# Weights-times-values products of even and odd key blocks accumulated in the two halves of the PSUM partitions

## The chip, the cores and the metric

One core of a Trainium2 chip runs the whole program. The metric is device time in microseconds (us) of one execution; the lower the better.

## The reference

One layer of a hybrid encoder trunk over 2048 positions of width 1024, all in float32. A combined input projection feeds three groups of heads (an mLSTM, a gated recurrence and a sparse attention); their outputs go through an output projection and a gated feed-forward net (FFN) with a short convolution. The change touches only the sparse attention, which is this, cut to what matters:

```python
def dsa_attention(q, k, v, iq, ik, iw):          # 4 heads x 64, blocks of queries
    rel = relu(einsum('bqhd,bsd->bqhs', iqb, ikf))
    score = einsum('bqh,bqhs->bqs', iwb, rel) * idx_scale      # the indexer
    score = where(admissible, score, -inf)                     # causal by chunks of 64
    top_val, top_idx = top_k(score, n_sel)                     # 256 keys of each query
    logits = einsum('bqhd,bqkhd->bqhk', qb, k[top_idx]) * att_scale
    p = softmax(where(valid, logits, -inf))
    return einsum('bqhk,bqkhd->bqhd', p, v[top_idx])
```

The kernel gathers no keys. It finds for each query the value of its 256th best score, adds a large negative number to the logits of all other keys, and takes the softmax over all keys up to the query's own block.

## The kernel before

**Work.** Queries come in 16 blocks of 128 (i = 0 to 15). Block i sees nk = i + 1 key blocks of 128, in chunks of up to four key blocks (512 keys). For each head h and chunk ci, `dsa_att` (L812) runs three steps:

- `scores`: TensorE multiplies queries by keys (`sd<-ks,aqh` and `sd<-ks,aql`), VectorE adds the mask and takes the maximum (L843), ScalarE takes the exponential in place in tile `L` (L855).
- `turn`: TensorE transposes the up to four 128x128 pieces of `L` through the identity matrix (`sd<-ident,L`, L55), ScalarE copies them to SBUF (`PT`, L866), and a DMA fetches the values `vs`.
- `values`: TensorE multiplies the transposed weights by the values. The stationary operand is `vs[:, k, :]`, 128 rows by 64 columns; the moving operand is 128 columns of `PT`; the result, 64 partitions by 128 columns, accumulates over all key blocks in the PSUM tile `av` (one buffer).

In `av`, heads 0 and 2 use partitions 0 to 63 and heads 1 and 3 use partitions 64 to 127, so that the four heads fill 128 partitions by 256 columns:

```python
p0, kn = (h % 2) * 64, min(4, nk - 4 * ci)
for k in range(kn):
    self.mm(av[p0:p0 + 64, (h // 2) * 128:(h // 2 + 1) * 128], vs[:, k, :], ...)
```

At a block's end ScalarE copies `av` to `ot` (L895), TensorE transposes it back in two 128x128 pieces (`sd<-ident,ot`), VectorE multiplies it by the inverse row sums into `oc` (L901), TensorE transposes `oc` in two pieces (`sd<-ident,oc`), and ScalarE copies the result to `hc` (L909), from where a DMA takes it to the concatenated head outputs `d_cat`.

**Order.** The order of TensorE's instructions is that of the program's text. The attention is a generator: each `yield` gives the time after which its next step may be issued, on a clock of the planner's own (`self.now`), which every call of `mm` (L48) and `tr` (L53) moves on. The big matrix products (`mm<-...`, in the projections, the output projection and the FFN) call `tick` between groups of products, and `tick` issues the next due step of one stream (norm, gates, lru, mlstm, att, score). The selection of the 256 best runs as two lanes of VectorE and ScalarE instructions (tiles `pl`, `cand`, `canda`), which are issued at a lower priority. The order on the other engines is set by a scheduler at build time.

**Words used below.** A burst is the row of `av` products that one call of `values` issues, one to four key blocks. Over the 16 blocks there are 4 x (1 + 2 + ... + 16) = 544 products in 160 bursts: 112 of four key blocks, 16 of three, 16 of two and 16 of one. L51 is the line of every matrix product and L55 that of every transpose.

Of the kernel before, what the change touches and what calls it, by code (L numbers as in the profile page):

```python
# [5 lines left out]
F32 = mybir.dt.float32  # L6
# [5 lines left out]
AF = mybir.ActivationFunctionType  # L12
OP = mybir.AluOpType
# [20 lines left out]
class Trunk:  # L34
# [787 lines left out]
    def dsa_att(self, i):  # L822
        nc, ap = self.nc, self.ap
        ve, ac = nc.vector, nc.scalar
        n = 128 * (i + 1)
        nk = i + 1
        nch = (nk + 3) // 4
        qh, ql = self.dsa_load(i, "a")
        madd = self.madd.pop(i) if i >= 2 else self.dsa_blank(i)
        sums = self.sm.tile([128, 4, 4], F32, name="sums")  # L830
        L, mx, PT = {}, {}, {}

        def scores(h, ci):
            c, w = 512 * ci, min(512, n - 512 * ci)
            if ci == 0:
                mx[h] = self.sm.tile([128, 4], F32, name="mx")
            L[h, ci] = ap.tile([128, 512], F32, name="L", bufs=4)
            ks = ap.tile([128, 512], F32R, name="ks", bufs=2)
            nc.sync.dma_start(ks[:, :w].bitcast(F32), self.d_ak[h * 128:(h + 1) * 128, c:c + w])
            ps = self.sd()  # L840
            self.mm(ps[:, :w], qh[:, h, :], ks[:, :w], True, False)
            self.mm(ps[:, :w], ql[:, h, :], ks[:, :w], False, True)
            ve.tensor_tensor_reduce(L[h, ci][:, :w], ps[:, :w], madd[:, c:c + w], 1.0, -3e38, OP.add, OP.max,  # L843
                                    mx[h][:, ci:ci + 1])
            if ci + 1 < nch:
                return
            nm = self.sm.tile([128, 1], F32, name="nmx")
            if nch > 1:
                ve.tensor_reduce(nm, mx[h][:, :nch], AX.X, OP.max)
                ve.tensor_scalar(nm, nm, -0.125, None, OP.mult)  # L850
            else:
                ve.tensor_scalar(nm, mx[h][:, 0:1], -0.125, None, OP.mult)
            for k in range(nch):
                w = min(512, n - 512 * k)
                ac.activation(L[h, k][:, :w], L[h, k][:, :w], AF.Exp, scale=0.125, bias=nm[:, 0:1],  # L855
                              accum_out=sums[:, h, k:k + 1])

        def turn(h, ci):
            kn = min(4, nk - 4 * ci)
            ps = self.sd()  # L860
            for k in range(kn):
                self.tr(ps[:, k * 128:(k + 1) * 128], L[h, ci][:, k * 128:(k + 1) * 128])
            vs = ap.tile([128, 4, 64], F32, name="vs", bufs=2)
            nc.sync.dma_start(vs[:, :kn, :], self.d_v[:, h, 4 * ci:4 * ci + kn, :])
            pt = ap.tile([128, 512], F32, name="PT", bufs=2)
            ac.activation(pt[:, :kn * 128], ps[:, :kn * 128], AF.Copy)  # L866
            PT[h, ci] = pt, vs

        def values(h, ci):
            pt, vs = PT[h, ci]  # L870
            p0, kn = (h % 2) * 64, min(4, nk - 4 * ci)
            for k in range(kn):
                self.mm(av[p0:p0 + 64, (h // 2) * 128:(h // 2 + 1) * 128], vs[:, k, :], pt[:, k * 128:(k + 1) * 128],
                        4 * ci + k == 0, 4 * ci + k == nk - 1)
        yield 4.0
        for ci in range(nch):
            scores(0, ci)
            yield 1.5 if ci + 1 < nch else 4.0
        av = self.ps.tile([128, 512], F32, name="av", bufs=1)
        before = None  # L880
        for h in range(4):
            for ci in range(nch):
                turn(h, ci)
                if h < 3:
                    scores(h + 1, ci)
                if before is not None:
                    values(*before)
                before = h, ci
                yield 3.5 if ci + 1 < nch else 4.5
        values(*before)  # L890
        rs = self.sm.tile([128, 4], F32, name="rsum")
        ve.tensor_reduce(rs, sums[:, :, :nch], AX.X, OP.add)
        ve.reciprocal(rs, rs)
        ot = ap.tile([128, 256], F32, name="ot", tag="PT", bufs=2)
        ac.activation(ot, av[:, :256], AF.Copy)  # L895
        yield 2.0
        ps = self.sd()
        for j in range(2):
            self.tr(ps[:, j * 128:(j + 1) * 128], ot[:, j * 128:(j + 1) * 128])
        oc = ap.tile([128, 4, 64], F32, name="oc", tag="rt", bufs=2)  # L900
        ve.tensor_tensor(oc, ps[:, :256].rearrange("p (h d) -> p h d", h=4), rs[:, :, None].to_broadcast([128, 4, 64]),  # L901
                         OP.mult)
        yield 2.5
        of = oc.rearrange("p h d -> p (h d)")
        ps = self.sd()
        for j in range(2):
            self.tr(ps[:, j * 128:(j + 1) * 128], of[:, j * 128:(j + 1) * 128])
        hc = ap.tile([128, 2, 128], F32, name="hc", tag="PT", bufs=2)
        ac.activation(hc.rearrange("p j t -> p (j t)"), ps[:, :256], AF.Copy)  # L909
        nc.scalar.dma_start(self.d_cat[768:1024, i * 128:(i + 1) * 128].rearrange("(j c) t -> c j t", c=128), hc)  # L910
        self.att_done = i + 1
        self.planes -= i >= 2
        yield 0.5
# [290 lines left out]
```

## Time and profile before

| what | value |
|---|---|
| median of three runs | 3078.3 us (3076.73 to 3080.96) |
| the profiled execution's own time | 3076.76 us |
| its span (first to last instruction) | 3075.0 us |
| TensorE (PE) busy | 2837.2 us, 92% |
| VectorE (DVE) busy | 1760.1 us, 57% |
| ScalarE (ACT) busy | 1708.6 us, 56% |
| GpSimd (POOL) busy | 888.7 us, 29% |

The table is read with the times beside it: a run lasts 1.8 us longer than the span of its instructions. PE is the row of matrix products and transposes; PEld is the row of the loads of their stationary operands, which may lie under the products. A matmul's end is modelled in the profile, so the distance from one start to the next tells what one costs in a row of equal ones, and not its own length.

### The profile page before, as it was taken

The page shows a single profiled execution, that of the slowest core. Times are in us where ns is not written, and L with a number is a line of the kernel's source. Part 1 is how long each engine was busy: PE and PEld are TensorE (multiplying, and loading weights), DVE is VectorE, ACT ScalarE, POOL GpSimd, SP SyncE. Part 2 cuts the span into 40 slices and gives each one's busy share as a digit, 9 for nine tenths or more (in the row PEclk, how much of TensorE's full clock was granted, in tenths as well). Part 3 has the DMA queues.
Part 4 walks back from the last instruction along what each step waited for, and adds up shares of the span by engine and source line. Part 5 has one row for each costly group of instructions (what it writes and reads, how often), then busy time and mean ns, then how long its engine had stood idle before and what let it go on. Part 6 is the DMA issues. An engine that isn't in the chain of part 4 may idle for free. (4 is left out here: it accounts for less than half of the span.)

```text
span 3075.0 us, 41708 instructions
## 1 busy us (share of the span) xinstructions
PE 2837.2 (92%) x13536; PEld 2300.5 (75%) x13536; DVE 1760.1 (57%) x3500; ACT 1708.6 (56%) x3427; POOL 888.7 (29%) x772
## 2 busy tenths in 40 slices
PE   8888898898887979988998999999999999999998
PEld 6776776787766767766776787768777777788886
DVE  3743475467538874687578853878643233443334
ACT  4785477665786449755974569356684323221112
POOL 4345455443456433434642000131100014010001
PEclk9999999999998989999998999999999999999999
DMA  6545544554455687774885556466666556575554
GB/s 192 149 119 159 147 126 127 148 143 112 129 155 150 206 219 243 253 230 153 287 266 195 190 187 191 148 184 234 195 216 197 174 161 229 179 270 193 192 191 157
DMA packets 468170, 568.61 MB, mean 185 GB/s; under 512 B 80096, under 2 KB 270560, under 8 KB 467952
## 3 DMA queue, kind: packets, MB, share of 16 engines
q1 hardware_dynamic: 426000, 513.44, 54.6%
q10 hardware_dynamic: 41952, 52.51, 5.0%
q8 instruction: 107, 1.75, 0.2%
q14 instruction: 111, 0.91, 0.1%
HBM read 444.09 MB, written 121.70 MB: 184 GB/s over the span
## 5 line engine op out<-in xcount | busy, mean ns | idle before, releaser
L209 POOL TENSOR_TENSOR wl<-wr,wh 128x512 fp32r<-128x512 f32 (+3 forms) x472 | 590.3, 1261 | 1269.0 <-ACT wh L203 577.1
L51 PE MATMUL mm<-hh,wh 128*128 128x512 f32 (+1 forms) x1920 | 778.1, 405 | 16.8 <-DVE stp L708 4.1
L51 PE MATMUL mm<-hh,wl 128*128 128x512 f32 (+1 forms) x1920 | 757.3, 394 | 0.0
L51 PE MATMUL mm<-hl,wh 128*128 128x512 f32 (+1 forms) x1920 | 757.0, 394 | 0.0
L1003 DVE SCALAR_TENSOR_TENSOR cu<-mm,fcw,cu 128x511 f32<-128x511 f32 (+1 forms) x352 | 260.8, 747 | 337.7 <-ACT cu L1001 332.6
L51 PEld LDWEIGHTS mm<-hh,wh 128*128 128x128 f32 (+1 forms) x1920 | 363.8, 190 | 108.7 <-issue 20.7
L51 PEld LDWEIGHTS mm<-hh,wl 128*128 128x128 f32 (+1 forms) x1920 | 363.3, 189 | 81.8 <-issue 0.4
L51 PEld LDWEIGHTS mm<-hl,wh 128*128 128x128 f32 (+1 forms) x1920 | 364.3, 190 | 71.5
L203 ACT ACTIVATE wh<-wr 128x512 fp32r<-128x512 f32 (+3 forms) x516 | 298.4, 589 | 200.1 <-PE mm L51 124.6
L1001 ACT ACTIVATE cu<-mm,fcb,fcw 128x512 f32<-128x512 f32 x176 | 135.8, 775 | 400.2 <-PE mm L51 375.7
L696 DVE TENSOR_SCALAR_CACHE_REDUCE pl<-pl,cand 128x384 bf16<-128x384 int16 (+13 forms) x217 | 306.2, 1411 | 5.7
L51 PE MATMUL mm<-wh,gh 128*128 128x512 f32 x684 | 283.0, 414 | 26.6 <-ACT fcar L1005 10.8
L718 ACT ACTIVATE pl<-pl,canda 128x512 bf16<-128x512 int16 (+13 forms) x217 | 294.5, 1357 | 21.8 <-DVE needa L776 10.0
L51 PE MATMUL mm<-wh,gl 128*128 128x512 f32 x684 | 275.0, 402 | 2.0 <-DVE gl L1032 2.0
L51 PE MATMUL mm<-wl,gh 128*128 128x512 f32 x684 | 275.0, 402 | 1.0 <-POOL wl L209 0.8
L123 POOL TENSOR_TENSOR rsy<-var,nhalf 128x1 f32<-128x1 f32 x64 | 39.6, 622 | 586.9 <-DVE var L141 494.9
L51 PE MATMUL mm<-wh,hh 128*128 128x384 f32 (+2 forms) x512 | 183.0, 357 | 23.9 <-ACT lg L614 12.1
L51 PEld LDWEIGHTS mm<-wh,gh 128*128 128x128 f32 x684 | 130.9, 191 | 67.6 <-ACT fcar L1005 15.5
L51 PE MATMUL mm<-wh,hl 128*128 128x384 f32 (+2 forms) x512 | 171.3, 335 | 2.4 <-DVE hl L179 2.4
L51 PE MATMUL mm<-wl,hh 128*128 128x384 f32 (+2 forms) x512 | 170.7, 333 | 0.0
L1065 DVE TENSOR_TENSOR y<-mm,y 128x512 f32<-128x512 f32 x144 | 97.4, 687 | 116.5 <-PE mm L51 114.4
L51 PEld LDWEIGHTS mm<-wh,gl 128*128 128x128 f32 x684 | 131.1, 192 | 35.1 <-DVE gl L1032 3.4
(306 smaller groups left out, 4753.7 us busy)
## 6 DMA issues: line engine op xcount, KB each, us to landing
wh<-d_w SPq DMA_DIRECT2D x391, 256.0 KB, 3.2
wl<-d_w SPq DMA_DIRECT2D x391, 256.0 KB, 3.2
d_w<-wh SPq DMA_DIRECT2D x132, 256.0 KB, 3.4
d_w<-wl SPq DMA_DIRECT2D x132, 256.0 KB, 3.4
ks<-d_ak SPq DMA_DIRECT2D x112, 256.0 KB, 4.0
wr<-in_ffn_up SPq DMA_DIRECT2D x176, 128.0 KB, 3.6
wr<-in_w_in SPq DMA_DIRECT2D x160, 128.0 KB, 2.5
wr<-in_w_in SPq DMA_DIRECT2D x96, 192.0 KB, 2.6
```

The costliest lines, as they stand in the source:

```text
L51: self.nc.tensor.matmul(out, a, b, start=start, stop=stop)
L123: self.pmark = self.nc.gpsimd.tensor_tensor(y, v, c, OP.pow)
L203: nc.scalar.activation(hi[:, :kk * n], raw[:, :kk * n], AF.Copy)
L209: eng.tensor_tensor(lo[:, :kk * n], raw[:, :kk * n], hi[:, :kk * n].bitcast(F32), OP.subtract)
L696: self.nc.vector.tensor_scalar(out[:, :n], src[:, :n], thr, None, OP.is_ge, OP.add, accum_out=cnt)
L718: self.nc.scalar.activation(out[:, :n], src[:, :n], AF.Sign, bias=bias, accum_out=s)
L1001: self.amark = nc.scalar.activation(u, ps, AF.Identity, scale=w[:, 2, j:j + 1], bias=self.fcb[:, j:j + 1])
L1003: self.dmark = nc.vector.scalar_tensor_tensor(u[:, d:], ps[:, :T - d], w[:, 2 - d, j:j + 1], u[:, d:], OP.mult, OP.add)
L1065: self.dmark = nc.vector.tensor_tensor(ys[i][:, c], o[i], ys[i][:, c], OP.add)
```

## The change

The two halves of the PSUM partitions no longer belong to heads but to key blocks: products of even k go to partitions 0 to 63 and those of odd k to partitions 64 to 127, each half accumulating on its own, and each head has 128 columns of `av` to itself. After the usual transposes the two halves stand side by side; each is multiplied by the inverse row sums and the second is added to the first. So `ot` is 512 columns wide, is transposed in four pieces, and VectorE has three instructions in place of one. With a single key block (block 0) the second half is set to zero. Two `yield` values grow, from 2.0 to 2.2 and from 2.5 to 3.2.

```diff
         def values(h, ci):
             pt, vs = PT[h, ci]
-            p0, kn = (h % 2) * 64, min(4, nk - 4 * ci)
-            for k in range(kn):
-                self.mm(av[p0:p0 + 64, (h // 2) * 128:(h // 2 + 1) * 128], vs[:, k, :], pt[:, k * 128:(k + 1) * 128],
-                        4 * ci + k == 0, 4 * ci + k == nk - 1)
+            for k in range(min(4, nk - 4 * ci)):
+                p0 = (k % 2) * 64
+                self.mm(av[p0:p0 + 64, h * 128:(h + 1) * 128], vs[:, k, :], pt[:, k * 128:(k + 1) * 128],
+                        4 * ci + k < 2, 4 * ci + k >= nk - 2)
...
-        ot = ap.tile([128, 256], F32, name="ot", tag="PT", bufs=2)
-        ac.activation(ot, av[:, :256], AF.Copy)
-        yield 2.0
+        ot = ap.tile([128, 512], F32, name="ot", tag="PT", bufs=2)
+        if nk == 1:
+            ve.memset(ot[64:128, :], 0.0)
+            ac.activation(ot[0:64, :], av[0:64, :], AF.Copy)
+        else:
+            ac.activation(ot, av, AF.Copy)
+        yield 2.2
         ps = self.sd()
-        for j in range(2):
+        for j in range(4):
             self.tr(ps[:, j * 128:(j + 1) * 128], ot[:, j * 128:(j + 1) * 128])
         oc = ap.tile([128, 4, 64], F32, name="oc", tag="rt", bufs=2)
-        ve.tensor_tensor(oc, ps[:, :256].rearrange("p (h d) -> p h d", h=4), rs[:, :, None].to_broadcast([128, 4, 64]),
-                         OP.mult)
-        yield 2.5
+        halves = ps.rearrange("p (h u d) -> p h u d", h=4, u=2)
+        rb = rs[:, :, None].to_broadcast([128, 4, 64])
+        ve.tensor_tensor(oc, halves[:, :, 0, :], rb, OP.mult)
+        o2 = ap.tile([128, 4, 64], F32, name="o2", tag="PT", bufs=2)
+        ve.tensor_tensor(o2, halves[:, :, 1, :], rb, OP.mult)
+        ve.tensor_tensor(oc, oc, o2, OP.add)
+        yield 3.2
```

What it moves: on TensorE a burst stands in the program as it did. These rows are those around the last burst of block 15, in the FFN, the same before and now (each row one or more instructions with their output's size; only the output's partitions differ, which a row doesn't show):

```order
L51 MATMUL mm<-hl,wh 128x512
L51 MATMUL mm<-hh,wl 128x512
L51 MATMUL av<-PT,vs 64x128 x4
L51 MATMUL mm<-hh,wh 128x512
L51 MATMUL mm<-hl,wh 128x512
```

Every one of the 160 bursts has as many products as before and stands apart from the others, with products or transposes of another kind on both sides. Behind that burst, still on TensorE, the end of block 15 reads so in the difference of the two programs:

```order
 L51 MATMUL mm<-hl,wh 128x512
 L51 MATMUL mm<-hh,wl 128x512
-L55 MATMUL sd<-ident,ot 128x128 x2
+L55 MATMUL sd<-ident,ot 128x128 x4
+L51 MATMUL mm<-hh,wh 128x512
+L51 MATMUL mm<-hl,wh 128x512
+L51 MATMUL mm<-hh,wl 128x512
```

The transposes of `ot` stay at their place and are four; six products (two such triples) move ahead of the transposes of `oc`. Counted in the 10176 `mm` products, the bursts and a block's end move by at most 18 from block 4 on, and later by up to 54 in blocks 2 and 3; the indexer's scoring steps of blocks 4 to 6 move by up to 60 either way.

On VectorE the end of block 15 read so before (`cu` and `gl` are tiles of the FFN's convolution and gate):

```order
L1028 TENSOR_TENSOR cu<-cu 128x512
L901 TENSOR_TENSOR oc<-sd,rsum 128x256
L1032 TENSOR_TENSOR gl<-cu,gh 128x512
L1003 SCALAR_TENSOR_TENSOR cu<-mm,fcw,cu 128x511
L1003 SCALAR_TENSOR_TENSOR cu<-mm,fcw,cu 128x510
```

and now (line numbers are 8 higher behind the change; `o_25058` is `o2`):

```order
L1036 TENSOR_TENSOR cu<-cu 128x512
L1040 TENSOR_TENSOR gl<-cu,gh 128x512
L907 TENSOR_TENSOR oc<-sd,rsum 128x256
L909 TENSOR_TENSOR o_25058<-sd,rsum 128x256
L910 TENSOR_TENSOR oc<-oc,o_25058 128x256
L1011 SCALAR_TENSOR_TENSOR cu<-mm,fcw,cu 128x511
```

The three instructions follow one another and stand one place later.

## Rows read from the trace of the kernel before

**Rows 1.** The page's busy times of TensorE and its weight loads.

```profile
span 3075.0 us, 41708 instructions
...
PE 2837.2 (92%) x13536; PEld 2300.5 (75%) x13536; DVE 1760.1 (57%) x3500; ACT 1708.6 (56%) x3427; POOL 888.7 (29%) x772
```

**Rows 2.** Busy us of each engine (instructions) in three stretches; then clock, DMA.

```profile
0.00:1200.00 1200.00, 1045.21 (x5356) 872.14 (x5357) 694.60 (x1554) 778.52 (x1635) 558.11 (x510) 0.94 0.56 156
1200.00:2500.00 1300.00, 1237.16 (x5780) 978.13 (x5779) 847.00 (x1568) 787.84 (x1538) 260.77 (x201) 0.98 0.64 207
2500.00:3075.00 575.00, 554.82 (x2404) 450.21 (x2402) 218.47 (x379) 142.23 (x256) 69.82 (x61) 0.99 0.58 197
```

**Rows 3.** Instructions on tile av: ns min/median/max, first and last start.

```profile
L51 PEld LDWEIGHTS av<-PT,vs x1088: 132/137/231, 101.4 to 2448.1; 128*64 128x64 f32 x182
L51 PE MATMUL av<-PT,vs x1088: 272/273/477, 101.4 to 2448.2; 128*64 128x128 f32 x182
L895 ACT ACTIVATE ot<-av x16: 357/384/393, 124.3 to 2448.6; 128x256 f32<-128x256 f32 x16
```

**Rows 4.** Timeline around one burst of four key blocks: start us, us, instruction, [idle before].

```profile
2388.24 0.60 PE L55 MATMUL sd<-ident,L 128*128 128x128 f32 x4
...
2388.57 0.19 PEld L51 LDWEIGHTS sd<-ks,aqh 128*128 128x128 f32 x1
...
2388.92 0.40 PE L51 MATMUL sd<-ks,aql 128*128 128x512 f32 x1
2388.94 0.60 ACT L866 ACTIVATE PT<-sd 128x512 f32<-128x512 f32 x1 [5.74 <-PE sd L55]
2389.24 0.85 PEld L51 LDWEIGHTS av<-PT,vs 128*64 128x64 f32 x8 [0.37 <-issue]
2389.25 1.09 PE L51 MATMUL av<-PT,vs 128*64 128x128 f32 x8
...
2390.26 0.19 PEld L51 LDWEIGHTS mm<-wh,gh 128*128 128x128 f32 x1 [0.17 <-DVE nmx L849]
2390.26 0.50 PE L51 MATMUL mm<-wh,gh 128*128 128x512 f32 x1
...
2390.60 0.39 PE L51 MATMUL mm<-wl,gh 128*128 128x512 f32 x1
2390.60 0.19 PEld L51 LDWEIGHTS mm<-wh,gl 128*128 128x128 f32 x1
```

**Rows 5.** Timeline around one burst of a single key block.

```profile
1851.37 0.43 PE L51 MATMUL av<-PT,vs 128*64 128x128 f32 x2
...
1851.74 0.50 PE L51 MATMUL mm<-hh,wh 128*128 128x512 f32 x1
```

**Rows 6.** The second weight load of the burst of rows 4.

```profile
2389.30 0.14 PEld L51 LDWEIGHTS av<-PT,vs 128*64 128x64 f32 x1
```

**Rows 7.** Who waited for whom: us in total, times, longest; TensorE's longest total first.

```profile
PE sd L55 <- ACT L L855: 50.0, 21, 7.2
PE sd L55 <- DMA mt<-d_m: 19.5, 6, 5.0
PE mm L51 <- ACT fcar L1005: 19.3, 11, 7.9
```

**Rows 8.** Timeline of block 15's end.

```profile
2448.56 0.39 ACT L895 ACTIVATE ot<-av 128x256 f32<-128x256 f32 x1 [0.30 <-PE av L51]
...
2451.25 0.38 PE L55 MATMUL sd<-ident,ot 128*128 128x128 f32 x2
...
2451.66 0.43 DVE L901 TENSOR_TENSOR oc<-sd,rsum 128x256 f32<-128x256 f32 x1 [0.81 <-PE sd L55]
...
2454.24 0.38 PE L55 MATMUL sd<-ident,oc 128*128 128x128 f32 x2
```

**Rows 9.** Timeline of block 13's end, where a lane's copy stands ahead.

```profile
2093.34 1.22 DVE L769 COPY pl<-sc 128x2048 int16<-128x2048 int16 x1
...
2094.47 0.42 DVE L901 TENSOR_TENSOR oc<-sd,rsum 128x256 f32<-128x256 f32 x1
...
2095.05 0.38 PE L55 MATMUL sd<-ident,oc 128*128 128x128 f32 x2
```

**Rows 10.** The page's group of the lanes' counts on VectorE.

```profile
L696 DVE TENSOR_SCALAR_CACHE_REDUCE pl<-pl,cand 128x384 bf16<-128x384 int16 (+13 forms) x217 | 306.2, 1411 | 5.7
```

## The prediction

> **What bounds the kernel now.** I read the busy times first, then the same by stretches, then what TensorE waits for. TensorE is busy 2837.2 of 3075.0 us, VectorE 1760.1 and ScalarE 1708.6 [rows 1]. By stretches TensorE is busy 1045.21 of 1200 us while the projections run (87%), 1237.16 of 1300 us in the FFN stretch that carries the later attention blocks (95%), and 554.82 of the last 575 us [rows 2]. The reader is to see that no other engine comes near. The waits say the same from the other side: TensorE's longest total is 50.0 us for the exponentials of the attention, in 21 pieces, the next are 19.5 and 19.3 us [rows 7]. So TensorE's order is the path nearly everywhere, and what a burst of `av` products takes off TensorE comes off the end, except just ahead of a wait.
>
> What a burst costs is read from its timeline. A call of `mm` with plain float32 operands is two passes on TensorE: 544 products leave 1088 passes [rows 3]. In a burst of four key blocks the eight passes reach from the first start to the end of the last in 1.09 us, one is 0.273 us long [rows 3, 4], so the last starts 0.82 us after the first. The weight loads give the pitch: eight in 0.85 us, each 0.137 [rows 3, 4], so 0.713 us between first and last start; the second starts 0.06 us after the first [rows 6], which leaves 0.653 us for six, 0.109 us each. The bursts agree among themselves: 1.01 us from the first `av` start to the next product for eight passes [rows 4], 0.37 for two [rows 5], 0.64 us for six passes more, 0.107 each with its rounding. So within a half the passes go one behind the other at 0.109 us, though a load of 64 columns takes only 0.06 us and lies under the pass before: the moving operand is what takes the time.
>
> A burst also has a price at both ends. The first load waits 0.37 us and the load behind the burst 0.17 us with the weight-load row idle [rows 4], whereas the load behind the four transposes, 128 columns wide, starts while these still run, with no idle shown. So TensorE treats the 64-column products as something apart and empties itself around them. The change keeps all 160 bursts, and this price with them.
>
> **The change part by part.** *The halves.* Two neighbouring products of a burst now write different halves of the partitions. Nowhere in the trace do they: a burst is of one head, so of one half, and two bursts never touch. What it is worth is therefore bounded. From below: nothing, if a pass waits for the pass before whatever its half (0.109 us as now), nor is a loss per pass to be expected, since count, shape and place of the passes stay. From above: the first pass of a product may run together with the last pass of the product ahead of it, as that one is in the other half; the second pass of a product is in the half of its own first and stays behind it. So a neighbour pair can save one pass, 0.109 us. There are 112 x 3 + 16 x 2 + 16 x 1 = 384 such pairs: 384 x 0.109 = 41.9 us. In between: if the load for the other half starts only when the pass ahead has started, the pair is 0.06 us apart, the distance of two loads [rows 6], and saves 0.05: 384 x 0.05 = 19 us. I take the upper bound, because loads already run ahead of their passes here, and because the emptying at both ends fits an array divided in two parts.
>
> [...]
>
> *What waits take back.* Where TensorE is not full, part of a saving turns into a longer wait. Blocks 0 to 7 have 96 of the 384 pairs, blocks 8 to 15 have 288; the first eight lie within the first 1200 us, the others in the FFN stretch. Weighted by the busy share, 0.25 x 0.87 + 0.75 x 0.95 = 0.93, so 41.9 becomes 39.0 us (an estimate).
>
> *The transposes.* Two more for each of 16 blocks. Four in a row take 0.60 us, one of them about 0.273 as the `av` passes of the same moving width, so 0.11 us a start [rows 3, 4]: 32 x 0.11 = 3.5 us added on TensorE.
>
> *The copy of `av`.* 512 columns in place of 256. The copy `PT` of that shape takes 0.60 us [rows 4], the present one 0.384 [rows 3]: 0.2 us more, 16 times, 3.5 us of ScalarE. In block 15 the copy ends at 2448.95 and the transposes start at 2451.25 [rows 8], 2.3 us that cover it. Uncovered it would cost those 3.5 us; I count nothing.
>
> *The merge.* Three VectorE instructions for one, 0.42 us each [rows 9], 16 x 0.84 = 13.4 us on an engine with 1300 us free. What could count is the delay ahead of the transposes of `oc`, behind which the products of the FFN queue on TensorE. In block 15 `oc` ends at 2452.09 and they start at 2454.24 [rows 8], 2.15 us of cover, to which the longer yield adds two product triples. In block 13 a lane's copy of 1.22 us stands ahead of `oc`, and the cover is 2095.05 - 2094.89 = 0.16 us [rows 9]. I count 2 us in all for such blocks. The memset of block 0 and its half-height copy are one instruction each, under the same cover.
>
> *The order.* The first blocks' steps move by up to 54 products, the later ones by 18 at most. That may bring or cost single waits like those of [rows 7], 2 to 4 us each, of either sign; I put nothing into the sum and some 6 us into the range.
>
> *The sum.* -39.0 + 3.5 + 2 = -33.5 us. Against the profiled execution, 3076.8 - 33.5 = 3043.3 us; the median of the runs lies 1.5 us above that execution, so **3045 us**.
>
> **The rivals.** *Loads one by one* (chance 0.14): the two halves overlap, but a load doesn't run ahead into the other half. 19 x 0.93 = 18, less 5.5 of costs, 12 to 13 us faster: 3066 us. For it speaks that each load shown starts with the pass ahead of it; against it nothing that this trace shows.
>
> *The halves don't overlap* (0.25): the change doesn't do what it says, and the costs stay: 3078.3 + 5.5 = 3084 us, at the border between no change and slower. For it speaks that a pass at 64 columns goes at 0.109 us although its load takes half of that, so the moving operand, which both halves would need at once from all 128 rows, may be the limit for both together. [...]
>
> *The merge comes late* (0.08): the other side. Nothing overlaps, and the three VectorE instructions end after TensorE reaches the transposes of `oc`. The point from which it decides is the cover of 0.16 to 2.15 us less 0.84 for the two added instructions: a single count of a lane, 1.41 us on the mean [rows 10], between the transposes of `ot` and the merge uses up what is left. At 1.41 us for each of 16 blocks it costs 22.6 us: 3084 + 23 = 3107 us. Against it speaks that the merge's three instructions follow one another in VectorE's order and that the longer yield leaves TensorE more to do before.
>
> **How the numbers follow.** The forecast, full overlap of neighbours, has 0.53, its own range is 3035 to 3056 us: below, all 41.9 us and a few waits fewer; above, half of the waits of [rows 7] behind attention steps longer by a burst's saving and an order a few waits worse. A difference of 0.2%, 6.2 us, is about what a measurement of this kernel can tell from no change. Faster: the forecast and the loads one by one, 0.67. The case without overlap lies at 3084 and is divided between the same and slower, 0.16 and 0.09; the late merge adds 0.08 to slower. The range of 3035 to 3084 us leaves out the late merge, half of the case without overlap and the tail of the forecast, some 0.2 to 0.25 together; I set its upper end at 3085 for this.
>
> **What would show it.** The timeline of a burst of four: from the first `av` start to the next product 1.01 us now, 0.68 if neighbours overlap, about 0.85 if the loads go one by one, 1.01 if nothing overlaps. Starts of neighbouring `av` passes of different products a few ns apart instead of 0.109 us. The transposes of `ot` as 32 more instructions at the same pitch. Waits of `sd L55` for `oc` no longer than a few us in total. The forecast is wrong if the bursts stay at 1.01 us, or if they shrink and TensorE's waits for the exponentials grow by as much.

## The result and the profile after

The changed kernel takes 3043.7 us (median of four runs, 3038.2 to 3046.2) against 3079.3 us of the kernel before in the same set of runs (3076.7 to 3081.0): a ratio of 0.9888, with an interval of 0.9875 to 0.9902. That is 35.6 us less. The prediction, 3045 us, is met.

The profiled executions are used for everything below. That of after took 3046.2 us, the longest of its four, and that of before was among its shortest. So their spans lie only 30.5 us apart, 3075.0 to 3044.5, and the ledger is made against this number. The page of after, to be read against [rows 1]:

```profile
span 3044.5 us, 41812 instructions
...
PE 2796.0 (92%) x13568; PEld 2251.8 (74%) x13568; DVE 1771.6 (58%) x3533; ACT 1710.8 (56%) x3429; POOL 885.9 (29%) x772
```

TensorE is busy 41.2 us less (2837.2 to 2796.0) and idle 10.7 us more (3075.0 - 2837.2 = 237.8, now 3044.5 - 2796.0 = 248.5). It is still the bound, by a wide margin.

The timeline of a burst of four key blocks in after, to be read against [rows 4]:

```profile
2352.68 0.40 PE L51 MATMUL sd<-ks,aql 128*128 128x512 f32 x1
2353.00 0.42 PEld L51 LDWEIGHTS av<-PT,vs 128*64 128x64 f32 x8 [0.37 <-issue]
2353.00 0.66 PE L51 MATMUL av<-PT,vs 128*64 128x128 f32 x8
...
2353.59 0.19 PEld L51 LDWEIGHTS mm<-wh,gh 128*128 128x128 f32 x1 [0.17 <-issue]
2353.59 0.50 PE L51 MATMUL mm<-wh,gh 128*128 128x512 f32 x1
```

From the first `av` start to the next product it is now 0.59 us, where it was 1.01. The idle time of the loads ahead of the burst (0.37) and behind it (0.17) is unchanged, as foretold. The same burst, asked for shorter pieces of the timeline, which count the passes that have started by then:

```profile
2353.00 0.33 PE L51 MATMUL av<-PT,vs 128*64 128x128 f32 x2
...
2353.00 0.44 PE L51 MATMUL av<-PT,vs 128*64 128x128 f32 x4
...
2353.00 0.55 PE L51 MATMUL av<-PT,vs 128*64 128x128 f32 x6
```

These are the pieces that end 0.03, 0.20 and 0.30 us after the burst's start. Passes come in twos: two at once, then two more, then two more. The eight starts lie at 0, 6, 160, 166, 269, 275, 378 and 385 ns. Since passes of one half lie at least 0.109 us apart in every burst of the kernel before, both passes of a product run beside both passes of its neighbour, not just one of them.

The groups of the `av` products, of the transposes of `ot` and of those of `oc` in after; the columns behind the bars are busy us, mean ns, and idle us ahead with what ended it:

```profile
L51 PE MATMUL av<-PT,vs 128*64 128x128 f32 x1088 | 100.1, 291 | 0.7 <-ACT fcar L1013 0.4 <-ACT PT L866 0.2
L55 PE MATMUL sd<-ident,ot 128*128 128x128 f32 x64 | 10.1, 283 | 3.5 <-ACT ot L897 3.1 <-ACT ot L899 0.4
L55 PE MATMUL sd<-ident,oc 128*128 128x128 f32 x32 | 6.3, 278 | 2.3 <-DVE oc L910 2.1 <-DVE stp L708 0.2
```

The same groups in the kernel before, 157.3 us for the `av` products and 6.4 us for 32 transposes of `ot`:

```profile
L51 PE MATMUL av<-PT,vs 128*64 128x128 f32 x1088 | 157.3, 285 | 0.0
L55 PE MATMUL sd<-ident,ot 128*128 128x128 f32 x32 | 6.4, 284 | 2.6 <-ACT ot L895 2.6
```

TensorE's waits in after, to be read against [rows 7]:

```profile
PE sd L55 <- ACT L L855: 45.6, 23, 6.9
PE mm L51 <- ACT fcar L1013: 23.3, 16, 6.6
PE sd L55 <- DMA mt<-d_m: 19.2, 5, 5.0
...
PE sd L55 <- ACT ot L897: 3.1, 1, 3.1
PE sd L55 <- DVE oc L910: 2.1, 2, 1.3
```

The waits for the exponentials did not grow (50.0 before, 45.6 now). The merge shows as 2.1 us in two waits. The 10.7 us of added idle time are what is left of many changes either way: the waits for the maximum `mx` grew most, by 6.5 us (5.8 to 12.3), those for the convolution's carry `fcar` grew by 4.0, others fell.

The end of block 15 in after, to be read against [rows 8]:

```profile
2419.37 0.60 ACT L899 ACTIVATE ot<-av 128x512 f32<-128x512 f32 x1 [0.17 <-PE av L51]
...
2422.16 0.60 PE L55 MATMUL sd<-ident,ot 128*128 128x128 f32 x4
...
2422.79 0.42 DVE L907 TENSOR_TENSOR oc<-sd,rsum 128x256 f32<-128x256 f32 x1 [0.61 <-PE sd L55]
...
2423.13 0.41 DVE L909 TENSOR_TENSOR o<-sd,rsum 128x256 f32<-128x256 f32 x1
...
2423.58 0.42 DVE L910 TENSOR_TENSOR oc<-oc,o 128x256 f32<-128x256 f32 x1
...
2426.70 0.38 PE L55 MATMUL sd<-ident,oc 128*128 128x128 f32 x2
```

The copy takes 0.60 us, as the copy of `PT` of the same shape had said, and ends at 2419.97, 2.19 us before the transposes need it. The merge ends at 2424.00, 2.70 us before the transposes of `oc`. In this block both are covered.

The last part is the clock. The line of the cores view, before and after:

```profile
core 0: 3075.0 us, clock 0.966
```

```profile
core 0: 3044.5 us, clock 0.963
```

What a lower mean clock costs is estimated here and below as its distance from 1 times the span, an upper estimate, since TensorE also waits in a part of the slow stretches (in that from 1957 us, shown at the end, it is busy 4.97 of 6.50 us). That is 0.034 x 3075.0 = 104.6 us before and 0.037 x 3044.5 = 112.6 us after, 8.0 us more.

**The ledger**, in us of the profiled executions (the forecast's terms as they stand in the prediction):

| term | foretold | found |
|---|---|---|
| passes that run beside others | -41.9 | -55.8 (256 pairs of products x 2 passes x 0.109) |
| transposes of `ot` | +3.5 | +3.7 (6.4 to 10.1) |
| waits, the merge's among them | +2.9 and +2 | +10.7 of idle time |
| clock | not foretold | +8.0 (the estimate above) |
| not placed | | +2.9 |
| sum | -33.5 | -30.5 |

The 256 pairs are 112 x 2 in the bursts of four and 16 each in those of three and two. The bursts taken one by one agree with them: their median, from the first start to the next product, went from 1.018 to 0.588 us for four key blocks, from 0.799 to 0.581 for three, from 0.581 to 0.369 for two, and stayed at 0.363 for one, which makes 55.0 us over all bursts.

### The profile page after: what moved, and what is told of

Read it like the earlier page. It is cut to its first block, busy times and chain, and to the rows that moved or that the text cites. A ratio compares the mean times of both kernels' runs of the same rounds, so it can differ in the third digit from the quotient of the medians.

```text
span 3044.5 us, 41812 instructions
## 1 busy us (share of the span) xinstructions
PE 2796.0 (92%) x13568; PEld 2251.8 (74%) x13568; DVE 1771.6 (58%) x3533; ACT 1710.8 (56%) x3429; POOL 885.9 (29%) x772
## 4 chain that ended last, share of the span: by engine, by line
PE 45%; DVE 13%; ACT 7%; DMA 7%; issue 4%; POOL 3%; SPq 1%; ACTq 0%; POOLq 0%; DVEq 0%
PE mm L51 40%; DVE pl L696 4%; PE sd L51 2%; PE sd L55 2%; ACT pl L718 2%; DVE cu L1011 2%; DMA xr<-d_x 1%; PE av L51 1%; DMA W<-d_c 1%; DVE cand L710 1%; ACT wh L203 1%; POOL y L975 1%; POOL wl L209 1%; DMA xr<-in_x 1%; POOL x L975 1%
```

## The experiments

After the result the theory was that the two halves are two queues of their own in TensorE, and that the total is what the bursts save less what the longer end of a block costs. The rivals were that only neighbours in program order overlap, that the two yields (the order) bring the gain or a good part of it, and that the end costs nothing. The first four kernels ran together (the kernel before has a median of 3079.8 us there), then four more (3078.0), then three (3079.0).

**e1: the products of one half next to one another.** After, with the even key blocks of a burst first.

```diff
-            for k in range(min(4, nk - 4 * ci)):
+            for k in sorted(range(min(4, nk - 4 * ci)), key=lambda k: k % 2):
```

> The changed kernel with the products of a burst issued half by half: key blocks 0, 2, 1, 3 in place of 0, 1, 2, 3. TensorE's order of all else is the same. Theory (only neighbours in the program overlap, pass by pass): in a burst of four only blocks 2 and 1 are neighbours of different halves, so one pair of passes or two overlap in place of four. The burst goes from 0.59 back to about 0.80 us (two pairs) or 0.91 (one), a burst of three likewise stays near 0.58 to 0.69, and the whole loses 112 x 0.21 to 0.32 = 24 to 36 us against the changed kernel, less what waits had taken: 3055 to 3075 us. Rival (TensorE looks ahead over the burst and pairs whatever stands in it): the burst stays at 0.59 us and the time at 3044 us within 6.

Measured: 3055.3 us (3051.5 to 3060.6), ratio 0.9918 (0.9900 to 0.9936). The timeline of a burst of four:

```profile
2358.05 0.42 PEld L51 LDWEIGHTS av<-PT,vs 128*64 128x64 f32 x8 [0.37 <-issue]
2358.05 0.66 PE L51 MATMUL av<-PT,vs 128*64 128x128 f32 x8
...
2358.65 0.50 PE L51 MATMUL mm<-wh,gh 128*128 128x512 f32 x1
```

Still 0.59 us (median 0.594), though four passes of the lower half now stand ahead of the first one of the upper. The starts again come in twos, 13 to 14 ns apart instead of 7; the pieces that end 0.03 and 0.20 us after the burst's start:

```profile
2358.05 0.34 PE L51 MATMUL av<-PT,vs 128*64 128x128 f32 x2
...
2358.05 0.45 PE L51 MATMUL av<-PT,vs 128*64 128x128 f32 x4
```

With 0.109 us at least between passes of one half, as in before, eight can start within 0.39 us only if the fifth pass of the program starts beside the first. So, by these pitches, the passes of this burst do not start in program order: the first of the upper half starts beside a pass that stands four places ahead of it. For the bursts the rival was right. The bursts cost 1.9 us more than in after (all 160, first start to next product: 91.4 us against 89.4). The median is 11.6 us above that of after (9 by the ratios), and so not explained by the bursts. TensorE's own order of instructions is that of after but for this swap; its idle time is 252.6 us against 248.5. That the total fell near what overlap of neighbours alone would have given is a coincidence.

**e2: the halves by chunk.** The new end of a block with bursts that stay in one half: chunk 0 below, chunk 1 above, and so on.

```diff
-            for k in range(min(4, nk - 4 * ci)):
-                p0 = (k % 2) * 64
+            p0, kn = (ci % 2) * 64, min(4, nk - 4 * ci)
+            for k in range(kn):
...
-                        4 * ci + k < 2, 4 * ci + k >= nk - 2)
+                        ci < 2 and k == 0, ci >= nch - 2 and k == kn - 1)
...
-        if nk == 1:
+        if nch == 1:
```

> The changed kernel with the halves given to chunks (even chunks of four key blocks below, odd ones above) in place of key blocks, so that all products of a burst are in one half; the wide copy, the four transposes, the three-part merge, the yields and TensorE's order stay. Blocks 0 to 3 have one chunk, so their second half is set to zero as in block 0. Theory (the gain is the overlap of neighbours): bursts of four go back to 1.02 us, and what is left is the change's cost, 3.5 us of transposes and about 2 of late merges: 3083 to 3087 us, no change or slightly slower than before. Rival (part of the gain comes from the order of the steps or the larger yields): under 3076 us with bursts of 1.02 us.

Measured: 3101.0 us (3091.6 to 3103.4), ratio 1.0062 (1.0042 to 1.0081), slower than before. The timeline of a burst of four, and the lines of the page and of the cores view:

```profile
2404.06 0.85 PEld L51 LDWEIGHTS av<-PT,vs 128*64 128x64 f32 x8 [0.37 <-issue]
2404.06 1.09 PE L51 MATMUL av<-PT,vs 128*64 128x128 f32 x8
...
2405.08 0.50 PE L51 MATMUL mm<-wh,gh 128*128 128x512 f32 x1
```

```profile
PE 2851.8 (92%) x13568; PEld 2308.5 (75%) x13568; DVE 1770.7 (57%) x3536; ACT 1713.8 (55%) x3429; POOL 884.2 (29%) x772
```

```profile
core 0: 3093.1 us, clock 0.963
```

The burst is back at 1.02 us: the gain is in the two halves side by side and in nothing else of the change. The new end and the new yields without it cost 21 us by the medians, 18.1 by the spans: 3.7 for the transposes, 3.5 of idle time (241.3 against 237.8), 9.9 by the clock estimate (114.4 against 104.6) and 1.0 not placed. That is more than the 5.5 us that the prediction put on the end, and above both expectations; e5 below puts 4 to 5 us of it on the yields. From here to after, which has the same order of instructions on TensorE and the same end (blocks 1 to 3 apart, which set their second half to zero here), it is 57 us by the medians and 54 by the ratios, as much as the bursts save.

**e3: the overlap alone.** The products as in after, and the end of a block as in before, with its yields. It leaves out heads 2 and 3 and the sum of the halves from block 1 on; block 0 is placed as in before. The edit is that against before.

```diff
-            p0, kn = (h % 2) * 64, min(4, nk - 4 * ci)
-            for k in range(kn):
-                self.mm(av[p0:p0 + 64, (h // 2) * 128:(h // 2 + 1) * 128], vs[:, k, :], ...
-                        4 * ci + k == 0, 4 * ci + k == nk - 1)
+            for k in range(min(4, nk - 4 * ci)):
+                p0, c0 = ((k % 2) * 64, h * 128) if nk > 1 else ((h % 2) * 64, (h // 2) * 128)
+                self.mm(av[p0:p0 + 64, c0:c0 + 128], vs[:, k, :], ...
+                        4 * ci + k < 2, 4 * ci + k >= nk - 2)
```

> The overlap alone: products as in the changed kernel, the end of a block as before (copy of 256 columns, two transposes, one VectorE instruction, old yields). It leaves out heads 2 and 3 and the sum of the halves from block 1 on, so its output is not the reference's; the instructions of the end are those of before. Theory (the merge costs little: 3.5 us of transposes and 2 of waits): 4 to 8 us faster than the changed kernel, 3036 to 3040 us. Rival (the merge's waits take back most of the 20 us by which the bursts' saving exceeds the measured gain): 3022 to 3032 us.

Measured: 3044.6 us (3037.9 to 3047.2), ratio 0.9879 (0.9860 to 0.9897). Both expectations were missed. The overlap brings 35 us by the medians and 37 by the ratio, of the 56 that the bursts save: TensorE is busy 2790.4 us, 46.8 less than before, and idle 251.2, 13.4 more. Its clock is 0.963. TensorE's instructions stand in the order of before, tile by tile, so these 13.4 us of idle time come without any move in its order. Here what is taken back goes with the overlap itself and not with the end of a block, against what e2 alone suggests.

**e5: the yields alone.** Before, with 2.2 for 2.0 and 3.2 for 2.5.

```diff
-        yield 2.0
+        yield 2.2
...
-        yield 2.5
+        yield 3.2
```

> The kernel before with nothing but the two larger yields (2.2 and 3.2). TensorE's order is then within 12 products of that of the changed kernel. Theory (the order is worth nothing by itself): 3079 us within 6. Rival (the moved steps of the early blocks bring or cost several waits): outside 3073 to 3085 us, by which the overlap's own part would be read anew.

Measured: 3084.4 us (3077.5 to 3090.4), ratio 1.0013 (1.0002 to 1.0024). Alone they lose 4 us (0.6 to 7.4 by the interval); they are not the gain.

**e6: the overlap with the new yields.** e3 and the two yields of e5; it leaves out what e3 leaves out.

> The overlap with the old end of a block (as in the run with the old end alone: heads 2 and 3 and the sum of the halves left out from block 1 on) but with the changed kernel's two larger yields, so that TensorE's order stands within 12 products of the changed kernel's. Theory (the wide copy, the transposes and the merge cost what the run by chunks showed, 19 us, and only the order hid this in the run with the old end): 3022 to 3028 us. Rival (with the bursts short the end costs only its 3.5 us of transposes and a little; the rest of the bursts' 57 us is lost to waits whatever the end): 3036 to 3042 us.

Measured: 3044.3 us (3038.7 to 3051.3), ratio 0.9880 (0.9862 to 0.9899). With the yields as they are in after, the end of a block costs next to nothing: 0.9888 against 0.9880, some 2.5 us as the ratios put it, with intervals that overlap nearly whole. The time lies above both expectations, 2 us above the rival's.

**e7: after with the old yields.**

```diff
-        yield 2.2
+        yield 2.0
...
-        yield 3.2
+        yield 2.5
```

> The changed kernel with the two yields as before (2.0 and 2.5), so the steps stand within 12 products of where they stood before the change. Theory (the larger yields cover the longer end of a block): slower than the changed kernel by 5 to 15 us, 3049 to 3059 us, with longer waits of the transposes of oc. Rival (the yields do nothing but shift the order): 3044 us within 6, and the waits for oc as they are.

Measured: 3060.2 us (3054.4 to 3063.2), ratio 0.9936 (0.9920 to 0.9952). The waits of TensorE:

```profile
PE sd L55 <- ACT L L855: 55.0, 23, 6.9
...
PE sd L55 <- DVE oc L910: 4.9, 2, 4.8
```

So in the changed kernel the yields are worth 16.5 us (15 by the ratios), as the theory had it. TensorE is busy 2797.5 us, as in after, and nearly the whole difference of the spans (16.9 us) is idle time, 263.9 against 248.5: 9.4 more for the exponentials, 2.8 more for the merge, the rest in small waits. Against e3, which has the same yields and the old end, the new end costs 15.7 us. The parts don't add, as the medians show:

| | old end, old yields | old end, new yields | new end, new yields | new end, old yields |
|---|---|---|---|---|
| no overlap | 3079 (before) | 3084 (e5) | 3101 (e2) | not run |
| overlap | 3045 (e3) | 3044 (e6) | 3044 (after) | 3060 (e7) |

With the overlap the new end costs 0 to 2.5 us with the new yields and 16 with the old; without the overlap it costs 17 with the new. The yields lose 4 us without the overlap, change nothing with it alone, and win 16 with it and the new end. The overlap itself brings 35, 40 or 57 us.

**e4: the planner told of the saving.** After, with its clock set back by what a pair of products saves, so that the steps behind are issued as late in real time as they were.

```diff
                 self.mm(av[p0:p0 + 64, h * 128:(h + 1) * 128], vs[:, k, :], ...
+            self.now -= 0.2176 * (min(4, nk - 4 * ci) // 2)
```

> The changed kernel with the planner's clock taking a pair of overlapped products as one (0.2176 us less for each pair of a burst). Theory (the planner's clock now runs ahead of TensorE, so steps are issued before their data are ready and TensorE waits): TensorE's idle time falls by some 10 us and the kernel comes to 3030 to 3038 us. Rival (the waits come from the other engines' queues and not from the planner's clock): 3044 us within 6; the many moved steps may shift it by a few us either way.

Measured: 3068.6 us (3061.3 to 3078.3), ratio 0.9971 (0.9960 to 0.9981). Neither expectation was met: a truer clock of the planner loses 25 us, with idle time of 271.2 us against 248.5 and a clock of 0.958. What is lost of the 56 us is not won back by a right price in the planner.

**e8: two chunks in a burst.** After, with the values of two chunks issued one behind the other, so that 80 bursts stand where 160 did (the expectation says 82; the trace has 80).

```diff
-        before = None
+        pend = []
...
+                if len(pend) == 2:
+                    values(*pend.pop(0))
+                    values(*pend.pop(0))
...
-                if before is not None:
-                    values(*before)
-                before = h, ci
+                pend.append((h, ci))
...
-        values(*before)
+        for p in pend:
+            values(*p)
```

> The changed kernel with the values of two chunks issued in one burst, half a step later: 82 bursts in place of 160. Theory (each burst pays for emptying TensorE at both ends: by the pitches before and behind it some 0.10 + 0.05 + 0.09 + 0.10 us): 78 x 0.3 = 23 us less, some of it lost to waits as with the change itself: 3022 to 3034 us. Rival (the price at the ends is hidden in the weight loads, or waits eat it): 3044 us within 6.

Measured: 3067.6 us (3059.7 to 3082.0), ratio 0.9970 (0.9945 to 0.9995). The page, a burst, and the waits:

```profile
span 3070.9 us, 41874 instructions
...
PE 2771.9 (90%) x13568; PEld 2259.9 (74%) x13568; DVE 1773.5 (58%) x3533; ACT 1712.9 (56%) x3427; POOL 893.6 (29%) x772
```

```profile
2418.00 1.09 PE L51 MATMUL av<-PT,vs 128*64 128x128 f32 x16
...
2419.02 0.66 PE L55 MATMUL sd<-ident,L 128*128 128x128 f32 x4
```

```profile
PE sd L55 <- DVE oc L912: 11.7, 1, 11.7
```

The price at the ends of a burst is real: 80 bursts fewer take 24.1 us off TensorE's busy time (2796.0 to 2771.9), 0.30 us each, and that at a lower mean clock (0.958 against 0.963). But idle time grows by 50.5 us (248.5 to 299.0), and one wait for the merge of a block alone is 11.7 us. The change in the order takes more than the bursts give, and the total is that of neither expectation.

**e9: yields larger still.** After, with 2.6 and 4.2.

```diff
-        yield 2.2
+        yield 2.6
...
-        yield 3.2
+        yield 4.2
```

> The changed kernel with still larger yields at a block's end (2.6 and 4.2 in place of 2.2 and 3.2). Theory (old yields lost 16 us because TensorE reached the end of a block before the merge was ready; the present ones cover it already, as the run without the merge was only 2 us faster): 3044 us within 6. Rival (the cover is still too small, and waits for oc and ot are part of the missing 20 us): 3030 to 3038 us.

Measured: 3089.8 us (3075.3 to 3103.6), ratio 1.0029 (1.0011 to 1.0048). The page and the waits:

```profile
span 3089.5 us, 41828 instructions
...
PE 2812.0 (91%) x13568; PEld 2263.9 (73%) x13568; DVE 1775.9 (57%) x3533; ACT 1722.0 (56%) x3434; POOL 886.1 (29%) x772
```

```profile
PE sd L55 <- POOL mo L590: 14.5, 4, 8.0
...
PE sd L55 <- DVE oc L910: 10.8, 3, 5.0
...
PE av L51 <- ACT PT L866: 9.1, 1, 9.1
```

Neither expectation was met. The longer yields do not even cover the merge (10.8 us against 2.1). TensorE also waits 14.5 us for `mo` (4.0 in after) and 9.1 for `PT` ahead of one burst (0.2). All of the gain is lost, though nothing was altered but the place at which steps are issued.

**e10: the values first.** After, with the products of the chunk before issued ahead of the transposes of this one.

```diff
+                if before is not None:
+                    values(*before)
...
-                if before is not None:
-                    values(*before)
```

> The changed kernel with a step's burst of values ahead of its transposes in place of behind them, so that the exponentials have 0.6 us more before TensorE asks for them; nothing else is altered in the program. Theory (what takes back some 20 us is spread over many small waits of the order, of which the waits for the exponentials, 46 us, are the largest): 2 to 8 us faster, 3036 to 3042 us. Rival (most of those waits are those of a block's first head, which has no burst to put ahead): 3044 us within 6.

Measured: 3074.5 us (3069.8 to 3084.3), ratio 0.9986 (0.9973 to 1.0000). Neither expectation was met, and the waits for the exponentials, which were to shrink, are 46.0 us against 45.6. TensorE waits little for `PT` itself (2.4 us ahead of the `av` products). Its idle time is 275.9 us, 27.4 more than in after, and the clock is the lowest of the profiled executions:

```profile
core 0: 3082.5 us, clock 0.954
```

**e11: how far apart in the program two passes that start together can stand.** e8, with the lower half's products of both chunks first, so that up to eight passes of one half stand ahead of the other's. It was run once.

```diff
-        def values(h, ci):
+        def values(h, ci, u):
...
-            for k in range(min(4, nk - 4 * ci)):
+            for k in range(u, min(4, nk - 4 * ci), 2):
...
+                    for u in range(2):
+                        for p in pend:
+                            values(*p, u)
```

> As the run with two chunks in one burst, but with all products of the lower half (key blocks 0 and 2 of both chunks) ahead of all of the upper half: up to eight passes of one half stand in the program before the first of the other. Theory (TensorE looks ahead over a few products, as four passes in the run half by half): the full burst of 16 passes stays near 1.03 us. Rival (it looks ahead no further than about four passes): the burst comes to 1.3 to 1.9 us, half of the passes or more going singly. The total time is not what this run is for.

Measured: 3083.5 us. A burst of 16 passes, the pieces of the timeline that end 0.48 and 0.54 us after its start, and the burst whole with the next product:

```profile
2441.70 0.65 PE L51 MATMUL av<-PT,vs 128*64 128x128 f32 x4
...
2441.70 0.82 PE L51 MATMUL av<-PT,vs 128*64 128x128 f32 x6
...
2441.70 1.58 PE L51 MATMUL av<-PT,vs 128*64 128x128 f32 x16
...
2443.21 0.66 PE L55 MATMUL sd<-ident,L 128*128 128x128 f32 x4
```

Four passes go alone, 160, 109 and 109 ns apart. Then comes one more and, 6 ns behind it, the first of a second row: by the pitch it is of the upper half, which begins ninth in the program, four places behind the pass that it starts beside. To the next product it is 1.51 us, against 1.02 in e8 for as many passes. The 0.49 us between them are four to five pitches of 0.109 us, so half of the 16 passes or somewhat more go alone (an estimate). That is what the rival had foretold, 1.3 to 1.9 us. Two independent queues without a limit on this distance would have kept the 1.02 us; the burst refutes that. Whether four places are a limit beyond this run was not shown. In after the other half always stands two passes behind.

## Why the prediction was right, point by point

**What bounds the kernel** was right. TensorE's busy time is 92% in both, and what the bursts gave up came off the end as far as the order let it.

**The halves overlap**: right, with a term mis-sized. The step that failed is "the first pass of a product may run together with the last pass of the product ahead of it". It runs together with the first pass already, two places ahead (6 to 7 ns behind its start), and e1 and e11 show passes that start beside one four places ahead (13 to 14 ns and 6 ns behind it). So each pair of products saves two passes and not each neighbour pair one, 55.8 us in place of 41.9. The foretold sign of 0.68 us for a burst of four came out as 0.59.

The trace of before has no neighbouring passes of different halves, so the overlap itself was the author's estimate. The bursts of after show it: of every two passes that start together one is saved whole, and what keeps a burst of four from half its time (0.588 us of 1.018) is what comes once in a burst, 203 ns from the last start to the next product among it. The two halves use the same 128 rows and yet start 6 to 7 ns apart, and so do their weight loads (7 ns between the first two of a burst of four, the median).

**The transposes** were right: 3.7 us for 3.5. **The copy** was right: 0.60 us, under 2.19 us of cover in block 15. **The merge** was right in the profile of after, 2.1 us of waits for the 2 foretold, but only with the yields of after: 4.9 in e7, 10.8 in e9.

**What waits take back** was too small: 2.9 us and the merge's 2 foretold, 10.7 us of idle time and 8.0 of clock found. The step that failed is the weighting by busy share, which takes waits as they stand and lets them grow in proportion; the clock was put at nothing without a reason. By stretches it reads so (busy us of each engine, then clock, DMA; the third ends with the kernel):

```profile
0.00:1200.00 1200.00, 1044.78 (x5406) 865.16 (x5407) 714.81 (x1580) 785.45 (x1647) 560.06 (x512) 0.94 0.56 157
1200.00:2500.00 1300.00, 1226.88 (x5888) 960.62 (x5887) 851.60 (x1595) 796.78 (x1552) 267.37 (x208) 0.98 0.65 208
2500.00:3045.00 545.00, 524.34 (x2278) 426.04 (x2276) 205.19 (x359) 128.54 (x231) 58.50 (x53) 0.99 0.60 201
```

Against [rows 2], the first 1200 us are as busy as they were (1044.78 for 1045.21) and the FFN stretch falls from 1237.16 to 1226.88, 95.2% to 94.4%, with 108 more of TensorE's instructions in it. No fixed share fits: with the same order on TensorE and the same end on both sides, the overlap brings 35 us in one case (before to e3), 40 in another (e5 to e6) and 57 in a third (e2 to after). Since e3 has the order of before, a part is taken back there by waits that fall otherwise in time and not by moved instructions.

**The order** was put at nothing, with 6 us in the range. That was the weakest step. Five kernels that have the same overlap and the same end, and differ in the order of issue alone (e4, e7, e9, e10, and e8 with its fewer bursts), lie 16 to 46 us above after. None lies below it. Among the orders tried, that of after is the best; whether it is the best there is was not tried.

The total was met by luck, because two errors of about 14 and 17 us cancel: the saving was put too low by 13.9, and what is taken back (idle time, clock and the unplaced rest, 21.6 for 4.9) by 16.7. The rivals without overlap and with single loads are refuted by the bursts. The late merge did not come in after, though e8 and e9 show that it lies close.

What stays open: which single waits make up the 10.7 us, and why one order is better than another. In e4 and e10 the added idle time is spread over several releasers, and none of them carries most of it. How much of the 8.0 us of clock is cause and how much an effect of the waits was not separated either.

## What to carry to other kernels

Here a row of products with a stationary operand of 64 columns was worth dividing between two halves of the PSUM partitions, with a cheap sum behind it: alternating, passes of the two halves started 6 to 7 ns apart, two cost what one had cost, and what TensorE was spared could be counted from the pitch of one burst (512 passes at 0.109 us). They still started together when they stood four places apart in the program (e1, e11). The price at the ends of such a burst stayed (0.37 and 0.17 us of idle time of the loads in the bursts shown, before and after), and an odd product out gained nothing: bursts of four, three, two and one key blocks lost 0.43, 0.22, 0.21 and 0 us. How much of this comes off the end is another matter, 35 to 57 us of 56. Where a planner interleaves several streams, judge such a change together with the planner's numbers, since here two yields decided over some 16 us of 36, and try the part alone both with the old and with the new numbers.

## What the runs showed of the hardware that was not expected

Passes of the two halves start in pairs, and not always in program order: 6 to 7 ns apart when alternating (after), 13 to 14 ns after a swap of two products (e1), and with eight of one half ahead not until the fifth pass, then 6 ns apart (e11).

A burst of 64-column products cost some 0.30 us beyond its passes here, measured by taking 80 bursts away (e8: 24.1 us of TensorE's busy time).

In one place the granted clock fell during a single wait. In after, TensorE waits for the convolution's carry between 1940 and 1964 us; the first row is that of the waits, and the others are busy times by stretches, with the granted clock in the third column from the end:

```profile
PE mm L51 <- ACT fcar L1013: 3.7, 2, 3.2
```

```profile
1940.00:1950.00 10.00, 10.00 (x45) 8.16 (x44) 9.89 (x19) 4.50 (x10) 2.57 (x2) 1.00 0.43 119
1950.00:1957.00 7.00, 4.82 (x22) 3.64 (x21) 6.96 (x13) 3.16 (x5) 1.28 (x1) 0.99 0.49 129
1957.00:1963.50 6.50, 4.97 (x11) 3.48 (x12) 6.39 (x17) 4.27 (x10) 0.00 (x0) 0.50 0.06 23
1963.50:1970.00 6.50, 6.50 (x36) 5.13 (x36) 6.46 (x9) 4.94 (x12) 4.32 (x3) 0.99 0.32 84
```

From 1940 to 1950 us, ahead of the wait, TensorE was busy without a gap at a granted clock of 1.00. The wait of 3.2 us ends at 1958.07, in the stretch with 0.50; taken by single microseconds the clock is 1.00 from 1955 to 1956, 0.92 in the next and 0.50 from 1957 on, so it fell while TensorE waited, and behind the stretch it is back at 0.99. The products of 512 columns start 0.23 us apart at 1953 us and 0.42 to 0.43 at 1961. Seven such steps in the stretch make 1.4 us more than at 0.23, beside the 3.2 us of the wait itself (an estimate). Over the profiled executions the mean clock tends to go down as idle time goes up: 0.966 in before (237.8 us idle), 0.963 in after (248.5), 0.958 in e4 (271.2), 0.954 in e10 (275.9). It doesn't follow it closely: 0.960 in e6 (245.0), and 0.958 in e8, which is idle longest (299.0).
